# Mixture-of-experts forward pass: paired weight loads, and the head of x loaded ahead of the section

## The chip, the cores and the metric

The kernel runs on one core of a Trainium2 chip. Its time is device time in microseconds (us), taken as the median of several executions. A profile comes from one further execution; its span runs from the first to the last instruction and is a little shorter than the device time (179.5 against 181.1 us here).

The engines that matter are TensorE (matmuls, "PE" in the profile, with its weight loads as "PEld"), VectorE ("DVE"), ScalarE ("ACT"), GpSimd ("POOL") and SyncE ("SP"). GpSimd and SyncE issue the transfers between HBM (the chip's main memory) and SBUF (the on-chip memory of 128 partitions). Matmul results land in PSUM, from which VectorE and ScalarE copy them.

## The reference

Eight experts, each a two-layer network on its own 256 tokens:

```python
n_experts, capacity, hidden, expert_hidden = 8, 256, 512, 2048
# x [8, 256, 512], w1 [8, 512, 2048], w2 [8, 2048, 512], all float32
h = np.matmul(x, w1)
h = np.maximum(h, 0)
return np.matmul(h, w2).astype(np.float32)
```

The weights are 67.1 MB, x and the output 4.2 MB each.

## The kernel before

The tuned kernel keeps four slots for w1 and four for w2 in SBUF. GpSimd issues all weight loads and lets the transfer cast them from fp32 to bf16. One load is the w1 or the w2 of one expert (2 MB of bf16, 4.19 MB read from HBM); only the w2 of the last expert is cut in halves. The first half-stage is the transposition of x on TensorE: x lies for that time in the slot which w2 of expert 2 takes later. A quarter of x, its head, goes through SyncE as fp32 and is cast by VectorE; the rest is loaded and cast by GpSimd's transfer.

Everything stands in one critical section, in which the kernel places its own semaphores:

```python
E, C, H = x.shape; F = w1.shape[2]       # 8, 256, 512; 2048
MC = C // P; K1 = H // P; K2 = F // P    # 2, 4, 16
NS = 4                                   # slots of w1, and of w2
GJ, UG = 4, 2; NG = K2 // GJ             # hidden columns go in groups of 4 blocks, two PSUM buffers

loads = []
for e in range(E - 1):
    loads += [(1, e, 0, 2), (2, e, 0, 2)]
loads += [(1, E - 1, 0, 2), (2, E - 1, 0, 1), (2, E - 1, 1, 1)]
d_w = [sem(f"d_w{i}") for i in range(len(loads))]

with tc.tile_critical(no_gpsimd_drain=True):
    sp = nc.sync
    sp.dma_start(x_head[:], x_v[:, :HEAD * H]).then_inc(d_head, 16)
    for i, (w, e, h, n) in enumerate(loads):      # SyncE passes landings on as credits
        sp.wait_ge(d_w[i], 16)
        if w == 1: sp.sem_inc(c_w1, 1)
        else:      sp.sem_inc(c_w2, n)
    sp.wait_ge(v_last, MC)
    sp.dma_start(out_v[:, E - 1, :], ...).then_inc(d_last, 16)

    pool = nc.gpsimd
    pool.dma_start(x_sb[:, HEAD * H:], x_v[:, HEAD * H:]).then_inc(d_x, 16)
    # [cut: identity]
    for i, (w, e, h, n) in enumerate(loads):
        old = e - NS
        if (w, e) == (2, 2):
            pool.wait_ge(p_xt, K1 * MC)           # x has been transposed
        if old >= 0 and h == 0:                   # the slot's old expert is done
            if w == 1: pool.wait_ge(p_h, NG * (old + 1))
            else:      pool.wait_ge(p_o, MC * (old + 1))
        if i == len(loads) - 1:
            pool.wait_ge(v_out, 1)
            pool.dma_start(out_v[:16, 0:5:2, :16], ...).then_inc(d_first, 16)
        # [cut: src and dst of this load]
        pool.dma_start(dst, src).then_inc(d_w[i], 16)
    pool.wait_ge(v_out, 2)
    pool.wait_ge(d_first, 16)
    pool.dma_start(out_v[:, :E - 1, :], ...).then_inc(d_out, 16)   # experts 0 to 6

    dve = nc.vector
    dve.memset(identity[:], 0.0).then_inc(s_zero)
    dve.wait_ge(d_head, 16)
    dve.tensor_copy(x_sb[:, :HEAD * H], x_head[:]).then_inc(s_cast)
    # [cut: copies of the transposes, and of each expert's output from o_ps to out_sb]

    act = nc.scalar
    # [cut: copies of transposes; ReLU of each group, h_ps to hT; last output copy]
    act.wait_ge(d_out, 16)
    act.wait_ge(d_last, 16)
```

TensorE runs a loop over the experts. An expert has a first pass (w1, in two rounds of a loop of 32 matmuls) and a second pass (w2, 32 matmuls). It takes one credit of w1 before the first pass and one credit of w2 before each half of the second:

```python
def expert():
    take(c_w1, 1)
    loop("half", reg["half"], 2, half)      # h_ps <- xT, w1
    for k in range(K2):
        if k % JH == 0:
            take(c_w2, 1)
        # [cut: addresses]
        for m in range(MC):
            ...                             # o_ps[m] <- w2, hT; the last of each m increments p_o
```

The next expert's first pass follows the last matmul of this one directly if its credit is there.

Of the kernel before, what the change touches and what calls it, by code (L numbers as in the profile page):

```python
# [8 lines left out]
FP32 = mybir.dt.float32  # L9
BF16 = mybir.dt.bfloat16  # L10
PE = mybir.EngineType.PE

FIRST_FREE = 16512


@with_exitstack
def kernel(
# [7 lines left out]
    nc = tc.nc  # L25
    P = 128
    E, C, H = x.shape
    F = w1.shape[2]
    MC = C // P
    K1 = H // P  # L30
# [4 lines left out]
    HEAD = 4  # L35

    NS = 4
# [3 lines left out]
    UG = 2  # L41
    NG = K2 // GJ

    JH = K2 // 2
# [4 lines left out]
    x_v = x.rearrange("e (pp r) k -> (e pp) (r k)", r=R)  # L49
    w1_v = w1.rearrange("e (p ko) n -> p e (ko n)", ko=K1)  # L50
    w2_v = w2.rearrange("e (p h j) n -> p e h (j n)", h=2, j=JH)
    out_v = out.rearrange("e (p mo) k -> p e (mo k)", mo=MC)


    places, free = {}, FIRST_FREE

    def allot(name, shape, dtype):
        nonlocal free
        places[name] = free
        t = nc.alloc_sbuf_tensor_at(name, shape, dtype, offset=free)  # L60
        free += math.prod(shape[1:]) * mybir.dt.size(dtype)
        return t

    w1_sb = allot("w1_sb", [P, NS, K1 * F], BF16)
    w2_sb = allot("w2_sb", [P, NS, K2 * H], BF16)
    xT = allot("xT", [P, K1, MC, E * P], BF16)
    hT = allot("hT", [P, K2, C], BF16)
    out_sb = allot("out_sb", [P, E, MC, H], FP32)
    x_head = allot("x_head", [P, HEAD * H], FP32)
    identity = allot("identity", [P, P], BF16)  # L70
    W1_AT, W2_AT, XT_AT = places["w1_sb"], places["w2_sb"], places["xT"]

    x_sb = w2_sb[:, 2, :]
    X_AT = W2_AT + 2 * K2 * H * 2
# [5 lines left out]
    def sem(name):  # L80
        return tc.alloc_semaphore(name)


    d_head, d_x = sem("d_head"), sem("d_x")
    d_first, d_out, d_last = sem("d_first"), sem("d_out"), sem("d_last")

    s_zero, s_ident, s_cast = sem("s_zero"), sem("s_ident"), sem("s_cast")
    p_xt, p_h, p_o = sem("p_xt"), sem("p_h"), sem("p_o")
    v_out, v_last = sem("v_out"), sem("v_last")

# [1 line left out]
    c_h, c_o, c_w1, c_w2 = sem("c_h"), sem("c_o"), sem("c_w1"), sem("c_w2")  # L92


    loads = []
    for e in range(E - 1):
        loads += [(1, e, 0, 2), (2, e, 0, 2)]
    loads += [(1, E - 1, 0, 2), (2, E - 1, 0, 1), (2, E - 1, 1, 1)]
    d_w = [sem(f"d_w{i}") for i in range(len(loads))]

    with tc.tile_critical(no_gpsimd_drain=True):  # L101


        sp = nc.sync
        sp.dma_start(x_head[:], x_v[:, :HEAD * H]).then_inc(d_head, 16)
        for i, (w, e, h, n) in enumerate(loads):
            sp.wait_ge(d_w[i], 16)
            if w == 1:
                sp.sem_inc(c_w1, 1)
            else:  # L110
                sp.sem_inc(c_w2, n)
        sp.wait_ge(v_last, MC)
        sp.dma_start(
            out_v[:, E - 1, :], out_sb[:, E - 1].rearrange("p m h -> p (m h)")
# [1 line left out]


        pool = nc.gpsimd
        pool.dma_start(x_sb[:, HEAD * H:], x_v[:, HEAD * H:]).then_inc(d_x, 16)  # L119
        pool.wait_ge(s_zero, 1)  # L120

        pool.affine_select(  # L122
            out=identity[:],
# [4 lines left out]
            pattern=[[-1, P]],  # L128
            channel_multiplier=1,
        ).then_inc(s_ident)  # L130
        for i, (w, e, h, n) in enumerate(loads):


            old = e - NS
            if (w, e) == (2, 2):
                pool.wait_ge(p_xt, K1 * MC)
            if old >= 0 and h == 0:
                if w == 1:
                    pool.wait_ge(p_h, NG * (old + 1))
                else:  # L140
                    pool.wait_ge(p_o, MC * (old + 1))
            if i == len(loads) - 1:


                pool.wait_ge(v_out, 1)
                pool.dma_start(  # L146
                    out_v[:16, 0:5:2, :16], out_sb[:16, 0:5:2, 0, :16]
                ).then_inc(d_first, 16)
            if w == 2:
                src = w2_v[:, e, h:h + n, :].rearrange("p h n -> p (h n)")  # L150
                dst = w2_sb[:, e % NS, h * JH * H:(h + n) * JH * H]
            else:
                src, dst = w1_v[:, e, :], w1_sb[:, e % NS, :]
            pool.dma_start(dst, src).then_inc(d_w[i], 16)  # L154
        pool.wait_ge(v_out, 2)
        pool.wait_ge(d_first, 16)
        pool.dma_start(  # L157
            out_v[:, :E - 1, :], out_sb[:, :E - 1].rearrange("p e m h -> p e (m h)")
        ).then_inc(d_out, 16)
        pool.drain()  # L160

# [5 lines left out]


        dve = nc.vector
        dve.memset(identity[:], 0.0).then_inc(s_zero)  # L172
        dve.sem_inc(c_xt[0], 1)
        dve.sem_inc(c_o, MC)
        dve.wait_ge(d_head, 16)
        dve.tensor_copy(x_sb[:, :HEAD * H], x_head[:]).then_inc(s_cast)  # L176
        for ko in range(K1):
            dve.wait_ge(p_xt, ko * MC + 1)
            copy_xt(dve.tensor_copy, ko, 0).then_inc(c_xt[0])
# [10 lines left out]

        act = nc.scalar
        act.sem_inc(c_xt[1], 1)
        act.sem_inc(c_h, UG)
        for ko in range(K1):
            act.wait_ge(p_xt, ko * MC + 2)
            copy_xt(act.copy, ko, 1).then_inc(c_xt[1])
# [9 lines left out]
                ).then_inc(c_h)  # L206
        act.wait_ge(p_o, E * MC)
        act.copy(out_sb[:, E - 1, 1, :], o_ps[1][:]).then_inc(v_last)  # L208
        act.wait_ge(d_out, 16)
        act.wait_ge(d_last, 16)  # L210

# [1 line left out]
        pe = nc.tensor  # L215

        def take(s, n):
            pe.wait_ge(s, n).then_inc(s, -n)  # L218

        def at(t, reg, free):  # L220
            row = math.prod(t.shape[1:])
            return mybir.RegisterAccessPattern(
                ap=[[row, P], *free],
                dtype=BF16,
                memsetref=f"{t.name}_set",
                regref=reg.name,
                is_regloc_offset=False,
                reg_ap_offset=reg.name,
                const_ap_offset=0,
                const_sub_tensor_id=0,  # L230
            )

        def matmul(dst, weights, moving, **flags):
            inst = mybir.InstMatmult(
                name=nc.get_next_instruction_name(),
                engine=PE,
                ins=[moving, weights],
                outs=[pe.lower_ap(dst)],
                tile_size=(P, P),
                tile_position=(0, 0),  # L240
                **flags,
            )
            return pe.add_instruction(inst)  # L243

        def loop(name, counter, times, body):
            head, end = f"{name}_head", f"{name}_end"
            nc.br(head, engines=[PE])
            with nc.body(head, valid_engines=[PE]):
                body()
                pe.br_lt(counter, times, on_true=head, on_false=end)  # L250
            nc.switch_bb(end)

        reg = {
            n: pe.alloc_register(n)
            for n in ["count", "half", "slot", "x", "b1", "b2"]
            + [f"xt{ko}" for ko in range(K1)]
            + [f"a{i}" for i in range(12)]
        }
        bank = [[reg[f"a{b * 6 + i}"] for i in range(6)] for b in range(2)]

        def last_column(step):

            return (P - 1) * step * 2

        count = reg["count"]

        n = MC * (R // MC)

        def transposes():
            i = 0  # L270
            for m in range(MC):
                take(c_xt[m], 1)
                for r2 in range(R // MC):
                    if i % 6 == 0:
                        for k in range(i, min(i + 6, n)):
                            row = (k % (R // MC)) * MC + k // (R // MC)
                            pe.reg_add(bank[i // 6 % 2][k - i], reg["x"], row * H * 2)
                        if i + 6 > n:
                            pe.reg_add(reg["x"], reg["x"], 2)
                            pe.reg_add(count, count, 1)  # L280
                    t = matmul(
                        xt_ps[m][:, r2, :],
                        at(w2_sb, bank[i // 6 % 2][i % 6], [[K1, P]]),
                        pe.lower_ap(identity[:]),
                        start_tensor_calc=True,
                        stop_tensor_calc=True,
                        is_transpose=True,
                    )
                    i += 1
                t.then_inc(p_xt)  # L290

        pe.wait_ge(s_ident, 1)
        pe.wait_ge(s_cast, 1)
        pe.wait_ge(d_x, 16)
        pe.reg_mov(count, 0)
        pe.reg_mov(reg["x"], X_AT + last_column(K1))
        loop("transposes", count, K1, transposes)
        for m in range(MC):
            pe.wait_ge(c_xt[m], 1)

# [30 lines left out]
        def first_addresses():  # L331
            a, b, regs = CHUNKS1[0]
            compute(address1, range(a, b), regs)
# [76 lines left out]
        for ko in range(K1):  # L410
            pe.reg_add(reg[f"xt{ko}"], count, XT_AT + ko * MC * E * P * 2)
        first_addresses()
        take(c_h, 1)
        loop("expert", count, E, expert)


# [28 lines left out]
```

## Time and profile before

The time is 181.12 us, the median of 3 executions (181.11 to 181.21).

| From the page | Value |
|---|---|
| Span | 179.5 us, granted TensorE clock 0.961 |
| VectorE, ScalarE, GpSimd busy | 9%, 22%, 7% |
| Weight loads, issued by GpSimd | 15 of 2 MB and 2 of 1 MB |
| GpSimd's queue, share of the 16 transfer engines' time | 96.9% |
| SyncE's queue (head of x, store of expert 7) | 2.3% |
| Chain that ended last | 9% of the span, expert 7's matmuls, then one ScalarE copy |

How to read the lines in the next section. In a line of the page or of the groups, "x15" is a count. In the page's rows of 40 slices, each digit is the busy share of one slice (4.5 us here) in tenths. A timeline line gives the start in us, the duration in us, the engine, the line of the kernel, the operation and its tiles, the count of merged instructions, and in brackets the idle time before and what ended it. A line with "DMA to landing" gives the time from a transfer's issue to its last byte's arrival. A line of a table of stretches gives the stretch, its length, the busy time of PE, PEld, DVE, ACT and POOL, the granted clock (1.00 is full), the share of the transfer engines and GB/s. GB/s counts bytes as written, so a casting load shows half of what it reads.

### The profile page before, as it was taken

What the parts mean: (1) busy time and instruction counts of PE and PEld (TensorE: products, weight loads), DVE (VectorE), ACT (ScalarE), POOL (GpSimd) and SP (SyncE); (2) the same over time, 40 slices, a digit from 0 to 9 for tenths busy, and PEclk for the clock granted to TensorE, in tenths of its full rate; (3) what the DMA queues carried; (4) which work ended last, traced back from release to release, by engine and by line L of the source; (5) the groups of instructions that cost most, each with busy time, mean ns of one, the idle gap of its engine ahead of it and who ended that gap; (6) DMA issues with size and microseconds to landing.
All of it is one profiled execution on the core that took longest, in us unless ns stands there. A gap on an engine that the chain in (4) does not pass through costs nothing. (4 is left out here: it accounts for less than half of the span.)

```text
span 179.5 us, 2103 instructions
## 1 busy us (share of the span) xinstructions
PE 130.4 (73%) x824; PEld 90.9 (51%) x832; DVE 15.9 (9%) x21; ACT 38.7 (22%) x38; POOL 11.7 (7%) x25
## 2 busy tenths in 40 slices
PE   0007659997949794949778698949894968769980
PEld 0007548746924493418633495428741963359630
DVE  0203420002000200020002000020002000200010
ACT  2002423500520044003500044003600350004410
POOL 7100030101010101010101000020000000002000
PEclk9999999999987999999999699996999999969999
DMA  5999999999999999999999999999999999999995
GB/s 186 261 203 226 230 208 204 234 215 197 230 226 212 204 230 215 197 234 226 193 223 230 208 204 234 215 197 230 226 212 204 230 215 201 230 201 211 351 423 217
DMA packets 3824, 40.37 MB, mean 225 GB/s; under 512 B 368, under 2 KB 368, under 8 KB 1392
## 3 DMA queue, kind: packets, MB, share of 16 engines
q0 software_dynamic: 3536, 38.80, 96.9%
q1 hardware_dynamic: 288, 1.57, 2.3%
HBM read 71.30 MB, written 4.20 MB: 421 GB/s over the span
## 5 line engine op out<-in xcount | busy, mean ns | idle before, releaser
L243 PE MATMUL h_ps<-xT,w_sb 128*128 x512 | 65.2, 292 | 17.1 <-PEq L218 17.1
L243 PEld LDWEIGHTS h_ps<-xT,w_sb 128*128 x512 | 59.5, 147 | 24.7 <-issue 21.7
L243 PE MATMUL o_ps<-w_sb,hT 128*128 x248 | 57.8, 387 | 11.0 <-PEq L218 10.6
L202 ACT ACTIVATE hT<-h_ps 128x1024 bf16<-128x1024 f32 x32 | 32.8, 1024 | 111.3 <-PE h_ps L243 111.3
L243 PEld LDWEIGHTS o_ps<-w_sb,hT 128*128 128x128 bf16 x256 | 24.9, 99 | 41.6 <-issue 14.0
L185 DVE COPY out_sb<-o_ps 128x512 f32<-128x512 f32 x15 | 9.7, 686 | 141.4 <-PE o_ps L243 141.4
L243 PE MATMUL xt_ps<-identity,w_sb 128*128 128x128 bf16 x64 | 7.6, 310 | 16.0 <-PEq L218 16.0
L243 PEld LDWEIGHTS xt_ps<-identity,w_sb 128*128 x64 | 6.5, 145 | 16.8 <-issue 16.8
L154 POOL DMA_DIRECT2D w_sb<-in_w_dram x17 | 9.1, 542 | 87.7 <-PE o_ps L243 34.5
L165 ACT COPY xT<-xt_ps 128x1024 bf16<-128x1024 bf16 x4 | 4.0, 1012 | 18.2 <-PE xt_ps L243 18.2
L165 DVE COPY xT<-xt_ps 128x1024 bf16<-128x1024 bf16 x4 | 4.9, 1224 | 11.9 <-PE xt_ps L243 11.9
L157 POOL DMA_DIRECT2D out_dram<-out_sb x1 | 0.9, 950 | 44.3 <-DMA out_dram<-out_sb 44.3
L208 ACT COPY out_sb<-o_ps 128x512 f32<-128x512 f32 x1 | 0.6, 586 | 5.9 <-PE o_ps L243 5.9
L146 POOL DMA_DIRECT2D out_dram<-out_sb x1 | 0.6, 557 | 20.0 <-DVEq L188 20.0
L176 DVE CAST w_sb<-x_head 128x2048 bf16<-128x2048 f32 x1 | 1.2, 1227 | 4.8 <-DMA x_head<-in_x_dram 4.8
L165 ACT ACT_TABLE_LOAD x1 | 1.3, 1283 | 1.1 <-SPq L101 1.1
L119 POOL DMA_DIRECT2D w_sb<-in_x_dram x1 | 0.7, 682 | 1.0 <-DVE identity L172 1.0
L122 POOL TENSOR_SCALAR_AFFINE_SELECT identity<-identity 128x128 bf16<-128x128 bf16 x1 | 0.3, 305 | 0.1
L172 DVE MEMSET identity<- 128x64 uint32 x1 | 0.1, 112 | 1.0 <-SPq L101 1.0
L429 POOL MEMSET const-float32-0.0<- 128x1 f32 x1 | 0.1, 99 | 0.2 <-issue 0.2
L429 POOL MEMSET const-bfloat16-1.0<- 128x1 bf16 x1 | 0.1, 102 | 0.0
L429 POOL MEMSET const-uint8-127<- 128x1 uint8 x1 | 0.1, 102 | 0.0
(1 smaller groups left out, 0.1 us busy)
## 6 DMA issues: line engine op xcount, KB each, us to landing
w_sb<-in_w_dram POOLq DMA_DIRECT2D x15, 2048.0 KB, 65.7
out_dram<-out_sb POOLq DMA_DIRECT2D x1, 3584.0 KB, 12.9
w_sb<-in_w_dram POOLq DMA_DIRECT2D x2, 1024.0 KB, 57.1
w_sb<-in_x_dram POOLq DMA_DIRECT2D x1, 1536.0 KB, 11.7
x_head<-in_x_dram SPq DMA_DIRECT2D x1, 1024.0 KB, 5.0
out_dram<-out_sb SPq DMA_DIRECT2D x1, 512.0 KB, 3.0
out_dram<-out_sb POOLq DMA_DIRECT2D x1, 3.0 KB, 44.8
```

Source lines behind the costliest of these rows:

```text
L119: pool.dma_start(x_sb[:, HEAD * H:], x_v[:, HEAD * H:]).then_inc(d_x, 16)
L122: pool.affine_select(out=identity[:], in_=identity[:], compare_op=mybir.AluOpType.not_equal, fill=1.0, base=0, pattern=[[-1, P]], channel_ ...
L146: pool.dma_start(out_v[:16, 0:5:2, :16], out_sb[:16, 0:5:2, 0, :16]).then_inc(d_first, 16)
L154: pool.dma_start(dst, src).then_inc(d_w[i], 16)
L157: pool.dma_start(out_v[:, :E - 1, :], out_sb[:, :E - 1].rearrange("p e m h -> p e (m h)")).then_inc(d_out, 16)
L165: return copy(xT[:, ko, m].rearrange("k (ep r2) -> k ep r2", r2=R // MC), xt_ps[m][:].rearrange("k r2 ep -> k ep r2"),)
L176: dve.tensor_copy(x_sb[:, :HEAD * H], x_head[:]).then_inc(s_cast)
L185: cp = dve.tensor_copy(out_sb[:, e, m, :], o_ps[m][:])
L202: act.activation(hT[:, g * GJ:(g + 1) * GJ, :].rearrange("p a c -> p (a c)"), h_ps[g % UG][:], mybir.ActivationFunctionType.Relu,).then_in ...
L208: act.copy(out_sb[:, E - 1, 1, :], o_ps[1][:]).then_inc(v_last)
L243: return pe.add_instruction(inst)
L429: nc = _bacc.Bacc("TRN2", target_bir_lowering=False, num_devices=1)
```

## The change

The change has five parts.

- The head of x is loaded and cast ahead of the critical section, as an ordinary tile under the Tile framework, which places the waits itself. GpSimd's own wait for it stands at the load that overwrites x.
- The weights of experts 0 to 5 go partly two experts per transfer: w1 and w2 of 0 and 1, w1 and w2 of 2 and 3, w1 of 4 and 5. That makes 12 weight loads instead of 17. A pair waits for the slot of its second expert, and both experts' credits come when the whole pair has landed.
- Landings are counted on one semaphore for each slot, and GpSimd's other transfers share one semaphore.
- The identity matrix is zeroed by GpSimd instead of VectorE.
- ScalarE's waits for the final stores stand last in the section, and TensorE begins with one ScalarE credit less instead of taking it.

Its purpose is fewer transfers, semaphores and instructions, and an earlier start of the first load. The arithmetic is unchanged.

```diff
-    loads = []
-    for e in range(E - 1):
-        loads += [(1, e, 0, 2), (2, e, 0, 2)]
-    loads += [(1, E - 1, 0, 2), (2, E - 1, 0, 1), (2, E - 1, 1, 1)]
-    d_w = [sem(f"d_w{i}") for i in range(len(loads))]
+    loads = []
+    for es in [(0, 1), (2, 3)]:
+        loads += [(1, es, 0, 2), (2, es, 0, 2)]
+    loads += [(1, (4, 5), 0, 2), (2, (4,), 0, 2), (2, (5,), 0, 2)]
+    for e in range(6, E - 1):
+        loads += [(1, (e,), 0, 2), (2, (e,), 0, 2)]
+    loads += [(1, (E - 1,), 0, 2), (2, (E - 1,), 0, 1), (2, (E - 1,), 1, 1)]
+    # [cut: landed[i], the semaphore and count of load i]
+    x_head = x_pool.tile([P, HEAD * H], FP32, tag="x_head")
+    nc.sync.dma_start(x_head[:], x_v[:, :HEAD * H])
+    nc.vector.tensor_copy(x_sb[:, :HEAD * H], x_head[:])
     with tc.tile_critical(no_gpsimd_drain=True):
         sp = nc.sync
-        sp.dma_start(x_head[:], x_v[:, :HEAD * H]).then_inc(d_head, 16)
-        for i, (w, e, h, n) in enumerate(loads):
-            sp.wait_ge(d_w[i], 16)
-            if w == 1:
-                sp.sem_inc(c_w1, 1)
-            else:
-                sp.sem_inc(c_w2, n)
+        for i, (w, es, h, n) in enumerate(loads):
+            sp.wait_ge(*landed[i])
+            sp.sem_inc((c_w1, c_w2)[w - 1], n * len(es) if w == 2 else len(es))
 # [cut]
         pool = nc.gpsimd
-        pool.dma_start(x_sb[:, HEAD * H:], x_v[:, HEAD * H:]).then_inc(d_x, 16)
-        pool.wait_ge(s_zero, 1)
+        pool.dma_start(x_sb[:, HEAD * H:], x_v[:, HEAD * H:]).then_inc(d_pool, 16)
+        pool.memset(identity[:], 0.0).then_inc(s_ident)
+        pool.wait_ge(s_ident, 1)
 # [cut]
-            old = e - NS
-            if (w, e) == (2, 2):
+            old = es[-1] - NS
+            if w == 2 and 2 in es:
+                tc.wait_critical_data_deps()
                 pool.wait_ge(p_xt, K1 * MC)
 # [cut]
+            e, ne, at_slot = es[0], len(es), es[0] % NS
             if w == 2:
-                src = w2_v[:, e, h:h + n, :].rearrange("p h n -> p (h n)")
-                dst = w2_sb[:, e % NS, h * JH * H:(h + n) * JH * H]
+                src = w2_v[:, e:e + ne, h:h + n, :].rearrange("p e h n -> p e (h n)")
+                dst = w2_sb[:, at_slot:at_slot + ne, h * JH * H:(h + n) * JH * H]
             else:
-                src, dst = w1_v[:, e, :], w1_sb[:, e % NS, :]
-            pool.dma_start(dst, src).then_inc(d_w[i], 16)
+                src, dst = w1_v[:, e:e + ne, :], w1_sb[:, at_slot:at_slot + ne, :]
+            pool.dma_start(dst, src).then_inc(landed[i][0], 16)
 # [cut]
-        act.sem_inc(c_h, UG)
+        act.sem_inc(c_h, UG - 1)
-        act.wait_ge(d_out, 16)
-        act.wait_ge(d_last, 16)
 # [cut]
-        take(c_h, 1)
         loop("expert", count, E, expert)
+        pool.drain()
+        act.wait_ge(d_pool, 48)
+        act.wait_ge(d_last, 16).then_inc(s_ident)
```

More of the change, by code (lines that the diff above doesn't have):

```diff
@@ L11 @@
 PE = mybir.EngineType.PE
-FIRST_FREE = 16512
+FIRST_FREE = 16512 + 8192
 @with_exitstack
@@ L68 @@
     out_sb = allot("out_sb", [P, E, MC, H], FP32)
-    x_head = allot("x_head", [P, HEAD * H], FP32)
     identity = allot("identity", [P, P], BF16)
@@ L81, in sem @@
         return tc.alloc_semaphore(name)
-    d_head, d_x = sem("d_head"), sem("d_x")
-    d_first, d_out, d_last = sem("d_first"), sem("d_out"), sem("d_last")
-    s_zero, s_ident, s_cast = sem("s_zero"), sem("s_ident"), sem("s_cast")
+    d_w1 = [sem(f"d_w1{i}") for i in range(NS)]
+    d_w2 = [sem(f"d_w2{i}") for i in range(NS)]
+    d_half, d_pool, d_last = sem("d_half"), sem("d_pool"), sem("d_last")
+    s_ident = sem("s_ident")
     p_xt, p_h, p_o = sem("p_xt"), sem("p_h"), sem("p_o")
@@ L95 @@
     loads = []
-    for e in range(E - 1):
-        loads += [(1, e, 0, 2), (2, e, 0, 2)]
-    loads += [(1, E - 1, 0, 2), (2, E - 1, 0, 1), (2, E - 1, 1, 1)]
-    d_w = [sem(f"d_w{i}") for i in range(len(loads))]
+    for es in [(0, 1), (2, 3)]:
[4 more added lines that the diff above has]
+    loads += [(1, (E - 1,), 0, 2), (2, (E - 1,), 0, 1), (2, (E - 1,), 1, 1)]
+    landed, counts = [], {}
+    for w, es, h, _ in loads:
+        s = d_half if h else (d_w1, d_w2)[w - 1][es[0] % NS]
+        counts[id(s)] = counts.get(id(s), 0) + 16
+        landed.append((s, counts[id(s)]))
+    x_pool = ctx.enter_context(tc.tile_pool(name="x_pool", bufs=1))
+    x_head = x_pool.tile([P, HEAD * H], FP32, tag="x_head")
+    nc.sync.dma_start(x_head[:], x_v[:, :HEAD * H])
+    nc.vector.tensor_copy(x_sb[:, :HEAD * H], x_head[:])
     with tc.tile_critical(no_gpsimd_drain=True):
         sp = nc.sync
-        sp.dma_start(x_head[:], x_v[:, :HEAD * H]).then_inc(d_head, 16)
-        for i, (w, e, h, n) in enumerate(loads):
-            sp.wait_ge(d_w[i], 16)
-            if w == 1:
-                sp.sem_inc(c_w1, 1)
-            else:
-                sp.sem_inc(c_w2, n)
+        for i, (w, es, h, n) in enumerate(loads):
+            sp.wait_ge(*landed[i])
+            sp.sem_inc((c_w1, c_w2)[w - 1], n * len(es) if w == 2 else len(es))
         sp.wait_ge(v_last, MC)
@@ L130 @@
         ).then_inc(s_ident)
-        for i, (w, e, h, n) in enumerate(loads):
-            old = e - NS
-            if (w, e) == (2, 2):
+        for i, (w, es, h, n) in enumerate(loads):
+            old = es[-1] - NS
+            if w == 2 and 2 in es:
+                tc.wait_critical_data_deps()
                 pool.wait_ge(p_xt, K1 * MC)
@@ L147 @@
                     out_v[:16, 0:5:2, :16], out_sb[:16, 0:5:2, 0, :16]
-                ).then_inc(d_first, 16)
+                ).then_inc(d_pool, 16)
+            e, ne, at_slot = es[0], len(es), es[0] % NS
             if w == 2:
-                src = w2_v[:, e, h:h + n, :].rearrange("p h n -> p (h n)")
-                dst = w2_sb[:, e % NS, h * JH * H:(h + n) * JH * H]
-            else:
-                src, dst = w1_v[:, e, :], w1_sb[:, e % NS, :]
-            pool.dma_start(dst, src).then_inc(d_w[i], 16)
+                src = w2_v[:, e:e + ne, h:h + n, :].rearrange("p e h n -> p e (h n)")
+                dst = w2_sb[:, at_slot:at_slot + ne, h * JH * H:(h + n) * JH * H]
+            else:
+                src, dst = w1_v[:, e:e + ne, :], w1_sb[:, at_slot:at_slot + ne, :]
+            pool.dma_start(dst, src).then_inc(landed[i][0], 16)
         pool.wait_ge(v_out, 2)
-        pool.wait_ge(d_first, 16)
+        pool.wait_ge(d_pool, 32)
         pool.dma_start(
             out_v[:, :E - 1, :], out_sb[:, :E - 1].rearrange("p e m h -> p e (m h)")
-        ).then_inc(d_out, 16)
-        pool.drain()
+        ).then_inc(d_pool, 16)
         def copy_xt(copy, ko, m):
@@ L171 @@
         dve = nc.vector
-        dve.memset(identity[:], 0.0).then_inc(s_zero)
         dve.sem_inc(c_xt[0], 1)
         dve.sem_inc(c_o, MC)
-        dve.wait_ge(d_head, 16)
-        dve.tensor_copy(x_sb[:, :HEAD * H], x_head[:]).then_inc(s_cast)
         for ko in range(K1):
@@ L279, in transposes @@
                             pe.reg_add(reg["x"], reg["x"], 2)
-                            pe.reg_add(count, count, 1)
                     t = matmul(
@@ L290, in transposes @@
                 t.then_inc(p_xt)
[L292 to L297, printed above, removed]
+        pe.wait_ge(s_ident, 2)
+        pe.wait_ge(d_pool, 16)
+        x_first = X_AT + last_column(K1)
+        pe.reg_mov(reg["x"], x_first)
+        loop("transposes", reg["x"], x_first + K1 * 2, transposes)
         for m in range(MC):
```

## The prediction

> **What bounds the kernel now.** I read the page first (shares of busy time, the 40 slices, the HBM line), then the TensorE timeline, then single weight loads with their time to landing, then a table of stretches for the tail.
>
> From the page:
>
> ```profile
> PE 130.4 (73%) x824; PEld 90.9 (51%) x832; DVE 15.9 (9%) x21; ACT 38.7 (22%) x38; POOL 11.7 (7%) x25
> DMA  5999999999999999999999999999999999999995
> HBM read 71.30 MB, written 4.20 MB: 421 GB/s over the span
> w_sb<-in_w_dram POOLq DMA_DIRECT2D x15, 2048.0 KB, 65.7
> ```
>
> No compute engine is full, but the DMA row is at 9 in every slice except the first and the last. The last line says how: a 2 MB weight load (4.19 MB of fp32 in HBM, cast on the way) lands a median 65.7 us after it was issued, so it waits in the queue behind six or so others. The queue never runs dry.
>
> From two single loads (the w1 loads of experts 5 and 7) and the TensorE timeline:
>
> ```profile
> L154 POOL DMA_DIRECT2D w_sb<-in_w_dram x1: 531/531/531, 50.1 to 50.1; - x1
> DMA to landing us min/median/max: 69.6/69.6/69.6
> ...
> L154 POOL DMA_DIRECT2D w_sb<-in_w_dram x1: 531/531/531, 88.8 to 88.8; - x1
> DMA to landing us min/median/max: 69.6/69.6/69.6
> ```
>
> ```profile
> 119.89 8.85 PE L243 MATMUL h_ps<-xT,w_sb 128*128 x64 [2.67 <-PEq L218]
> 129.53 7.07 PE L243 MATMUL o_ps<-w_sb,hT 128*128 x31 [0.79 <-PEq L218]
> 139.23 7.38 PE L243 MATMUL h_ps<-xT,w_sb 128*128 x64 [2.63 <-PEq L218]
> 148.91 7.07 PE L243 MATMUL o_ps<-w_sb,hT 128*128 x31 [2.31 <-PEq L218]
> 158.64 8.94 PE L243 MATMUL h_ps<-xT,w_sb 128*128 x64 [2.66 <-PEq L218]
> 167.47 7.07 PE L243 MATMUL o_ps<-w_sb,hT 128*128 x31
> ```
>
> Issue plus time to landing gives 50.1 + 69.6 = 119.7 us and 88.8 + 69.6 = 158.4 us. TensorE starts those experts 0.2 us later, at 119.89 and 158.64. Four loads lie between, so one takes 38.7 / 4 = 9.69 us (433 GB/s of reads). An expert costs 19.4 us of transfer but only about 14.5 us of TensorE (7.38 + 7.07), so TensorE starts each half the moment its weights land.
>
> The tail, by stretches (the two last columns are the DMA share and GB/s):
>
> ```profile
> 168.00:176.00 8.00, 6.54 (x30) 2.74 (x28) 0.69 (x1) 1.23 (x2) 0.00 (x0) 1.00 1.02 419
> 176.00:178.00 2.00, 0.00 (x0) 0.00 (x0) 0.00 (x0) 0.00 (x0) 0.00 (x0) 1.00 0.71 289
> ```
>
> The last half of w2 lands at 119.2 + 49.0 = 168.2 us. From there the transfers stay full to 176 us with the stores of experts 0 to 6, and the store of expert 7 follows at once: issued at 175.18, landed 3.0 us later at 178.2. So the chain of waits, which ends in TensorE and a ScalarE copy, misleads: behind expert 7's matmuls the transfers are still busy with 3.67 MB of other stores. The kernel is one unbroken stream of transfers from about 2 to 178 us, plus about 1.3 us of closing barrier.
>
> **What the Trainium skill says.** "DMA: Bandwidth & Descriptors", section "Where 436 GB/s comes from", puts the ceiling of the 16 ports at 435 GB/s; the 433 GB/s above agrees, so the stream has no room. Its section "Issuing engines are not separate DMA queues" says that SyncE's and GpSimd's transfers share the same 16 engines; the tail agrees, as expert 7's store runs when the others end. Its section "Latency and other measured facts" reports half the rate for copies between HBM tensors when neighbouring rows lie 4 MiB apart. The paired loads alternate between two experts 4 MiB apart; no run here shows whether that counts. "TensorE: Matmul & The Clock Gate", Part 1, says that an idle window of about 3.4 us halves the clock until about 3.4 us of work have passed. The trace agrees in size: a slow first pass takes 8.9 us instead of 7.38, but it also occurs after idle times of only 2.7 us, and not after all of them.
>
> **The change, part by part.**
>
> (1) Head of x by Tile, ahead of the section. SyncE now issues this load before the section's opening handshake. In the trace it left at 0.95 us, after a no-op and a branch which released the other engines at about 0.8 us. I take 0.2 us off. Everything in the stream stands behind this load, so all landings move 0.2 us earlier. The price is that TensorE, ScalarE, VectorE and SyncE now enter the section when the head has landed and VectorE has cast it (5.9 + 1.2 = 7.1 us). TensorE has nothing to do before the rest of x has landed (1.4 + 11.7 = 13.1 us), so this costs nothing. GpSimd does not wait at entry, only before the w2 load that overwrites x, where it waits for the transposes anyway. The identity's zeroing moves to GpSimd (0.1 us on VectorE), behind its first DMA issue; the weights it delays need not start before about 12.5 us. Value: -0.2 us.
>
> (2) Pairs. Seventeen weight issues become twelve, at about 0.54 us each on an engine busy 7%: nothing. Bytes and order are the same apart from the swap inside a pair. Counting 9.69 us a load from x at 13.1, and without the shift: w1 of 0 and 1 lands at 32.5 (expert 0 had it at 22.9), w2 of 0 and 1 at 51.9, w1 of 2 and 3 at 71.3, their w2 at 90.6, w1 of 4 and 5 at 110.0, w2 of 4 at 119.7, of 5 at 129.4, then as before: 139.1, 148.7, 158.4, 163.3, 168.2.
>
> TensorE then: expert 0 first pass 32.7 to 41.6 (slow clock), second pass 52.1 to 60.8; expert 1 has all its weights, 61.0 to 75.5; expert 2 first pass 75.6 to 83.0, wait, second pass 90.8 to 99.5 (slow clock, 8.75 as at 52 us in the kernel before). From there it has a backlog and works at 14.6 us an expert (7.38 + 7.07 and an estimated 0.15 for the turn): expert 3 ends at 114.1, 4 at 128.7, 5 at 143.3, 6 at 157.9. Expert 7 can't start before its w1 at 158.4 + 0.2. So the backlog of about 10 us is worked off with some 0.7 us to spare. If TensorE is late by one or two us there, its clock stays up and expert 7 takes 7.38 instead of 8.94 us, which pays 1.6 us back.
>
> Buffers: the pair of w1 4 and 5 waits for expert 1's first pass, about 68.3 us, while the queue has work to 90.6: 22 us in hand, the tightest case. w2 of 6 waits for expert 2's end, 99.5 against 139.1; w2 of 7 for expert 3's, 114.1 against 158.4. The stream doesn't break. Value: 0.
>
> (3) Credits per expert, one starting credit less, and a shared semaphore for GpSimd's transfers: the same waits in other bookkeeping. Value: 0.
>
> (4) ScalarE waits last. Its two waits end at the same landing at 178.2; one branch after them goes away. Value: -0.1 us.
>
> Sum: 181.12 - 0.2 - 0.1 = 180.8 us.
>
> **The rivals.**
>
> (A) The late start of TensorE costs. For it: the first matmul of an expert moves from 25.4 to 32.7 us, the second pass from 34.3 to 52.1. Were TensorE the bound, that would add 7 to 10 us. Against it: 19.4 against 14.6 us an expert, four experts to catch up in, and 1.6 us from the clock. Moreover the stream ends at 178 whatever TensorE does, as long as expert 7's store has been issued by about 175.2. If my turn is too short (say 16 us an expert), expert 7 starts near 164 and ends near 178.6: about 185 us.
>
> (B) The paired loads run slower, because a partition's two rows lie 4 MiB apart. For it: the skill's page. Against it: that figure is for every partition's row 4 MiB away from its neighbour's; here partitions stay 32 KB apart and only the two blocks of 32 KB in one partition are far apart. And the store of seven experts is such a form itself (7 pieces for each partition) and ran at 419 GB/s. Ten loads of 9.69 us are in pairs; 3% on those is 2.9 us, 184 us.
>
> (C) TensorE finishes earlier, since its clock stays up before expert 7, and the time falls by 1.6 us. Against it: the stores of the tail are in the same stream; an earlier store of expert 7 only shares the engines with the others. The tail stretch leaves 0.29 x 2.0 = 0.6 us of idle DMA at most: 180.3 us.
>
> (D) Larger transfers run closer to the peak. Against it: landings are already evenly spaced at 433 GB/s, with the next load always queued. Nothing to gain.
>
> **Range and chances.** The stream leaves little room down: 0.3 us for the start and end, up to 0.5 from the tail. Upwards, A and B in small form give up to 1 us. So 80% between 180.2 and 181.9 us. Faster by over 2% would need 177.5 us, below what the bytes allow: 2%. Slower by over 2% needs 184.7 us, so A or B in full: 5%. Within 2%: 93%.
>
> **What would show it.** Head of x issued at about 0.75 us; w1 of 7 landing near 158.2 us; the DMA row at 9 throughout; TensorE waiting long (about 10 and 8 us) before the second passes of experts 0 and 2, then hardly at all from 91 to 157 us, and shortly before expert 7; seven-expert store issued near 164 us. I am wrong if the w1 of 7 lands later than in the kernel before (B), if expert 7 starts well after its weights (A), or if the stream has a hole.

## The result, and the profile after

| | Time, us (median, range) | Ratio to before, 95% interval |
|---|---|---|
| Before | 181.12 (181.04 to 181.81) | |
| Changed | 180.61 (180.51 to 180.84) | 0.9967 (0.9952 to 0.9983) |

The changed kernel is 0.5 us, 0.3%, faster. Predicted were 180.8 us.

From the page of the changed kernel:

```profile
PE 129.4 (72%) x832; PEld 90.5 (51%) x832; DVE 15.8 (9%) x20; ACT 38.7 (22%) x38; POOL 10.3 (6%) x21
DMA  6999998999999999899899999999989999999995
HBM read 71.30 MB, written 4.20 MB: 422 GB/s over the span
w_sb<-in_w_dram POOLq DMA_DIRECT2D x5, 4096.0 KB, 48.0
w_sb<-in_w_dram POOLq DMA_DIRECT2D x5, 2048.0 KB, 51.0
```

The DMA row still has no hole. Some digits are 8, but the rate (422 against 421 GB/s) is what counts: the transfers are as full as before.

The start, from the timelines of the kernel before (two lines) and of the changed kernel (two lines), and the changed kernel's w1 load of expert 7 (its issue, and its time to landing):

```profile
0.95 0.38 SPq L105 DMA_DIRECT2D x_head<-in_x_dram  x1
1.44 0.68 POOL L119 DMA_DIRECT2D w_sb<-in_x_dram  x1 [1.00 <-DVE identity L172]
0.74 0.38 SPq L116 DMA_DIRECT2D x_head<-in_x_dram  x1
1.24 0.68 POOL L131 DMA_DIRECT2D w_sb<-in_x_dram  x1 [0.79 <-POOLq L440]
```

```profile
L169 POOL DMA_DIRECT2D w_sb<-in_w_dram x1: 528/528/528, 107.1 to 107.1; - x1
DMA to landing us min/median/max: 51.0/51.0/51.0
```

The head of x leaves at 0.74 instead of 0.95 us. The w1 of expert 7 lands at 107.1 + 51.0 = 158.1 instead of 158.4 us.

TensorE's timeline:

```profile
32.39 9.24 PE L252 MATMUL h_ps<-xT,w_sb 128*128 x64 [9.20 <-PEq L227]
51.74 9.73 PE L252 MATMUL o_ps<-w_sb,hT 128*128 x32 [10.11 <-PEq L227]
61.30 7.35 PE L252 MATMUL h_ps<-xT,w_sb 128*128 x64
68.54 7.07 PE L252 MATMUL o_ps<-w_sb,hT 128*128 x32
75.44 7.34 PE L252 MATMUL h_ps<-xT,w_sb 128*128 x64
90.44 9.15 PE L252 MATMUL o_ps<-w_sb,hT 128*128 x32 [7.66 <-PEq L227]
99.43 7.34 PE L252 MATMUL h_ps<-xT,w_sb 128*128 x64
...
113.57 7.35 PE L252 MATMUL h_ps<-xT,w_sb 128*128 x64
120.80 7.07 PE L252 MATMUL o_ps<-w_sb,hT 128*128 x32
127.70 7.35 PE L252 MATMUL h_ps<-xT,w_sb 128*128 x64
...
149.07 7.07 PE L252 MATMUL o_ps<-w_sb,hT 128*128 x32
158.22 8.85 PE L252 MATMUL h_ps<-xT,w_sb 128*128 x64 [2.08 <-PEq L227]
166.96 7.07 PE L252 MATMUL o_ps<-w_sb,hT 128*128 x32
```

It shows a wait of 9.2 us for the first pair, the two long waits before second passes (10.1 and 7.7 us, in the brackets), then lines without brackets, which are back-to-back work on the backlog, and a wait of 2.1 us before expert 7. With its weights there, an expert takes 127.70 - 113.57 = 14.13 us.

The tail, in the stretches of the prediction:

```profile
168.00:176.00 8.00, 6.03 (x28) 2.53 (x26) 0.69 (x1) 0.72 (x2) 0.00 (x0) 1.00 1.03 422
176.00:178.00 2.00, 0.00 (x0) 0.00 (x0) 0.00 (x0) 0.00 (x0) 0.00 (x0) 0.65 0.53 215
```

In 168 to 176 us the stores run at much the same rate as before (422 against 419 GB/s), and they finish a little sooner: 215 instead of 289 GB/s are left in the last stretch.

### The profile page after: what moved, and what is told of

It is laid out like the page before. It is cut to its first block, busy times and chain, and to the rows that moved or that the text cites. A ratio compares the mean times of both kernels' runs of the same rounds, so it can differ in the third digit from the quotient of the medians.

```text
span 178.9 us, 2103 instructions
## 1 busy us (share of the span) xinstructions
PE 129.4 (72%) x832; PEld 90.5 (51%) x832; DVE 15.8 (9%) x20; ACT 38.7 (22%) x38; POOL 10.3 (6%) x21
## 5 line engine op out<-in xcount | busy, mean ns | idle before, releaser
L252 PE MATMUL o_ps<-w_sb,hT 128*128 x256 | 61.3, 401 | 17.8 <-PEq L227 17.8
L252 PE MATMUL h_ps<-xT,w_sb 128*128 x512 | 62.2, 284 | 11.3 <-PEq L227 11.3
L252 PEld LDWEIGHTS h_ps<-xT,w_sb 128*128 x512 | 58.4, 146 | 15.9 <-issue 13.1
L252 PEld LDWEIGHTS o_ps<-w_sb,hT 128*128 128x128 bf16 x256 | 25.6, 102 | 50.7 <-issue 24.5
L169 POOL DMA_DIRECT2D w_sb<-in_w_dram x12 | 7.4, 619 | 105.1 <-PE h_ps L252 58.0
```

Of the source, the lines that this page charges most:

```text
L169: pool.dma_start(dst, src).then_inc(landed[i][0], 16)
```

## The experiments

Each run was compared with the kernel before on the same chip. My theory was the stream of transfers: what doesn't move its start, its length or the closing doesn't move the time. The rivals were TensorE, and the pairs themselves. One result, that of the first experiment, needed a further theory.

| Run | Time, us | Before, us | Ratio, 95% interval |
|---|---|---|---|
| Head of x alone | 181.96 | 181.12 | 1.0039 (1.0025 to 1.0053) |
| Pairs alone | 181.03 | 181.12 | 0.9996 (0.9990 to 1.0003) |
| Waits at the end alone | 181.17 | 181.12 | 1.0001 (0.9993 to 1.0009) |
| Changed, less TensorE work | 180.68 | 181.12 | 0.9977 (0.9970 to 0.9984) |
| Changed, two more pairs | 186.23 | 181.07 | 1.0281 (1.0261 to 1.0302) |
| Before, head issued late | 182.41 | 181.07 | 1.0070 (1.0053 to 1.0087) |
| Head and credit | 181.01 | 181.13 | 0.9994 (0.9988 to 1.0001) |
| Before, one TensorE wait more | 182.22 | 181.13 | 1.0054 (1.0038 to 1.0069) |
| Changed, bf16 store | 180.61 | 181.13 | 0.9970 (0.9963 to 0.9977) |
| Changed, pairs undone | 180.76 | 181.08 | 0.9981 (0.9974 to 0.9988) |
| Changed, waits put back | 180.88 | 181.08 | 0.9990 (0.9981 to 0.9998) |
| Changed, 22 semaphores more | 180.81 | 181.08 | 0.9986 (0.9978 to 0.9995) |

### Is the end set by TensorE or by the transfers?

Less TensorE work, in the changed kernel. Seven of 16 blocks of every second pass are left out, so this is not the full computation:

```diff
                 for m in range(MC):
+                    if k % 2 and k != K2 - 1:
+                        continue
                     mm = matmul(o_ps[m][:], ...)
```

> The changed kernel, leaving out the matmuls of 7 of the 16 blocks in every second pass (14 of 32 matmuls, 3.0 us of TensorE for each expert); its output is therefore not the reference's. TensorE ends near 171 instead of 174 us and the store of expert 7 is issued near 171.7 us. My theory (the transfers set the end): time 180.3 to 180.6 us. Rival (the chain of waits is right and TensorE's last expert sets the end): 177.6 us.

Measured: 180.68 us. The last two TensorE lines and the last store of its timeline, then its store line from the page (the last column is us to landing), and below them the same store in the changed kernel:

```profile
158.02 8.65 PE L252 MATMUL h_ps<-xT,w_sb 128*128 x64 [5.64 <-PEq L227]
166.56 4.05 PE L252 MATMUL o_ps<-w_sb,hT 128*128 x17
...
171.26 0.35 SPq L125 DMA_DIRECT2D out_dram<-out_sb  x1
```

```profile
out_dram<-out_sb SPq DMA_DIRECT2D x1, 512.0 KB, 6.4
```

```profile
174.67 0.35 SPq L125 DMA_DIRECT2D out_dram<-out_sb  x1
...
out_dram<-out_sb SPq DMA_DIRECT2D x1, 512.0 KB, 3.1
```

Expert 7's store leaves at 171.26 instead of 174.67 us, 3.4 us sooner, and then takes 6.4 instead of 3.1 us to land, beside the other stores (which land 0.5 us later than in the changed kernel, at 177.0 us). It lands at 177.6 us, much as in the changed kernel (177.8). The chain of waits of the page named the last matmuls and was wrong: they are not what the end hangs on.

Two more pairs, in the changed kernel:

```diff
-    loads += [(1, (4, 5), 0, 2), (2, (4,), 0, 2), (2, (5,), 0, 2)]
-    # [cut: w1 and w2 of expert 6, w1 of expert 7]
+    loads += [(1, (4, 5), 0, 2), (2, (4, 5), 0, 2)]
+    loads += [(1, (6, 7), 0, 2), (2, (6,), 0, 2)]
```

> The changed kernel with two more pairs: w2 of experts 4 and 5, and w1 of experts 6 and 7. The bytes and the stream's length stay. By the model with which I predicted: w2 of 4 and 5 lands near 129.0 us, so expert 4's second pass starts there (slow clock, to 138.4); experts 5 and 6 follow without a pause to 152.6 and 166.8, expert 7 to 181.0 us; its store is issued at 181.6 and lands at 184.7, time 187.4 us. Rival (only the stream sets the end, whatever TensorE does): 180.6 us.

Measured: 186.23 us. Its timeline:

```profile
129.03 0.58 PE L251 MATMUL o_ps<-w_sb,hT 128*128 x1 [8.39 <-PEq L226]
129.83 7.62 PE L251 MATMUL o_ps<-w_sb,hT 128*128 x30 [0.22 <-issue]
137.29 7.35 PE L251 MATMUL h_ps<-xT,w_sb 128*128 x64
...
172.80 7.07 PE L251 MATMUL o_ps<-w_sb,hT 128*128 x31
...
180.51 0.35 SPq L124 DMA_DIRECT2D out_dram<-out_sb  x1
```

So TensorE does set the end once a pair comes too late to work off its delay. The whole delay comes from the first of the two pairs, w2 of 4 and 5: after the wait of 8.4 us for it there is no further wait. Expert 4's second pass starts at 129.03 us as computed. The model was 1.1 us too slow in that pass alone: I had it end at 138.4 us by the slow clock, and the next pass began at 137.29. The three experts behind it took 14.2 us each (137.29 to 179.87 us), as expected here.

### What sets the start of the stream?

The kernel before, with the head issued late:

```diff
         dve.memset(identity[:], 0.0).then_inc(s_zero)
+        dve.memset(out_sb[:, 0:6]..., 0.0).then_inc(s_late)
# ...
+        sp.wait_ge(s_late, 1)
         sp.dma_start(x_head[:], x_v[:, :HEAD * H]).then_inc(d_head, 16)
```

> The kernel before, with the head's load made to wait for a zeroing of the output buffer on VectorE, which delays its issue by some 3 to 6 us. The zeroing is overwritten later. If the head alone sets the start of the stream and GpSimd's first transfer follows it, the hole is filled as soon as GpSimd's data can flow: the end moves by the time from 1.9 us to GpSimd's first packet. If GpSimd's queue is ready about 1 us after its issue ended (near 3 us), the time is about 182.2 us; if it isn't ready before 4.85 us, where its packets began in the kernel before, about 184 us. Rival (the start doesn't matter): 181.1 us.

Measured: 182.41 us. Two lines of its timeline, SyncE's and TensorE's first pass of expert 0:

```profile
7.58 0.38 SPq L107 DMA_DIRECT2D x_head<-in_x_dram  x1
...
37.55 9.99 PE L246 MATMUL h_ps<-xT,w_sb 128*128 x64 [1.88 <-PEq L221]
```

The head left 6.6 us late, and expert 0 started 12 us later than in the kernel before, but the time rose by only 1.3 us. In the trace, GpSimd's first packet moved at 2.83 us, where the head's had moved at 1.95: 0.9 us. The rows of the first 5 us, in slices of 0.125 us, first of the kernel before and then of this run:

```profile
DMA  0000000000000009993083959769699796969999
DMA  0000000000000000000000999967000000509999
```

The last landing came 1.1 us later. So 0.9 of the 1.3 us are the later first packet of the stream, whoever sends it. What the remaining 0.4 us are stays open (the second row also has a hole from about 3.5 to 4.3 us). TensorE's start, 12 us later, can have cost no more than these.

### The parts alone

The head of x alone, with the identity zeroed by GpSimd:

```diff
-        sp.dma_start(x_head[:], x_v[:, :HEAD * H]).then_inc(d_head, 16)
+    x_head = x_pool.tile([P, HEAD * H], FP32, tag="x_head")
+    nc.sync.dma_start(x_head[:], x_v[:, :HEAD * H])
+    nc.vector.tensor_copy(x_sb[:, :HEAD * H], x_head[:])
```

> The kernel before with one part of the change: the head of x loaded by Tile ahead of the section (and the identity zeroed by GpSimd, which goes with it); weights stay one expert per transfer. My theory (one unbroken stream of transfers, whose start this load sets): head issued near 0.74 us instead of 0.95, w1 of expert 7 landing near 158.1 instead of 158.4 us, time 180.8 to 180.9 us, 0.2 to 0.3 below before. Rival (the gain comes from the pairs): 181.1 us.

Measured: 181.96 us, 0.8 above before, which neither theory had. Yet the head left at 0.74 us, w1 of expert 7 landed at 158.1 us, and the span was shorter: a median of 179.1 against 179.3 us. The loss lies behind the span. Time less span is 2.86 us, against 1.78 in the kernel before. The list of transfers after the span's end shows two that carry instructions, of 16 and 8 KB; the kernel before has none there.

The pairs alone, the same lines of the diff as in the change:

> The kernel before with the pairs alone; the head of x, the identity and the waits at the end stay as before. My theory: TensorE starts expert 0 near 32.7 us instead of 25.4 and catches up before expert 7; w1 of 7 lands within 0.15 us of before; time 181.0 to 181.1 us. Rival (fewer, larger transfers shorten the stream): 180.8 us or less. Rival (two experts 4 MiB apart slow the loads): above 181.5 us.

Measured: 181.03 us, not told apart from before by this run. TensorE started expert 0 at 32.46 us and was waiting again for expert 7, which it began at 158.30 us. No sign of slower pairs.

The waits at the end alone:

```diff
         loop("expert", count, E, expert)
+        pool.drain()
+        act.wait_ge(d_out, 16)
+        act.wait_ge(d_last, 16).then_inc(s_ident)
```

> The kernel before with only GpSimd's drain and ScalarE's two waits moved to the end of the section. My theory: everything up to the last landing is unchanged, one branch less after it: time 181.0 us, 0.1 below before. Rival (the whole gain of the end comes from there): 180.8 us.

Measured: 181.17 us. The span is 0.1 us shorter (median 179.2), but the time behind it is 0.15 us longer (1.93), so nothing is left.

### The microsecond behind the span

The head alone adds one instruction each to the programs of TensorE, SyncE and ScalarE, and three to GpSimd's: 129 in the listing of TensorE's program instead of 128. The changed kernel has 127. The credit that TensorE no longer takes saves one. A second one goes by a part of the change that its list doesn't name: the loop over the transposes counts with its address register, so that no separate counter is set. I added the credit to the head alone:

```diff
-        act.sem_inc(c_h, UG)
+        act.sem_inc(c_h, UG - 1)
# ...
-        take(c_h, 1)
         loop("expert", count, E, expert)
```

> The run with the head of x alone, plus the credit of the change (ScalarE gives one credit less at the start and TensorE doesn't take it): one TensorE instruction less, as many as in the kernel before; SyncE and GpSimd keep their one and three instructions more than before. The head alone gave a span 0.2 us shorter but a time 0.8 us longer, and its trace has an instruction transfer of 16 KB after the span that the kernel before hasn't. Theory (TensorE's program grew by one instruction over a boundary of its instruction memory, and the end of the program pays for it): the extra microsecond goes, time 180.7 to 180.9 us. Rival (SyncE's or GpSimd's program, or Tile's tile itself, costs it): 181.9 to 182.0 us.

And, in the kernel before, one TensorE wait that has nothing to wait for:

```diff
         pe.wait_ge(s_cast, 1)
+        pe.wait_ge(s_zero, 1)
         pe.wait_ge(d_x, 16)
```

> The kernel before with one redundant TensorE wait, on a semaphore that has long been reached; nothing else changes, and it stands before the transposes where TensorE waits for x anyway. Theory (instruction memory of TensorE): span as before, 179.3 to 179.5 us, time 182.0 to 182.2 us, 0.9 to 1.1 more. Rival: 181.1 us, as before.

Measured: 181.01 us with the credit, 182.22 us with the needless wait. The span of the latter is 179.3 us as a median, as before; time less span is 2.87 us. The list of transfers of this kernel from 179.6 to 183 us, behind its span (queue, kind, count, MB, share):

```profile
DMA packets 2, 0.02 MB, mean 7 GB/s; under 512 B 0, under 2 KB 0, under 8 KB 0
q8 instruction: 1, 0.02, 2.4%
q14 instruction: 1, 0.01, 0.9%
```

The same stretch of the kernel before, from 179 us on:

```profile
DMA packets 0, 0.00 MB, mean 0 GB/s; under 512 B 0, under 2 KB 0, under 8 KB 0
```

The 129th TensorE instruction costs 1.09 us, and it comes with a fetch of 16 KB of instructions behind the span, which takes 1.33 us in this trace (1.43 us in that of the head alone). The twelve other kernels have no transfer there, and 1.7 to 1.9 us behind their spans. That the time waits for this fetch is the reading that fits; no run separates the two. The Trainium skill, "Runtime: NRT & Kernel Launch", section "Instruction fetch mechanics", has blocks of 16 KiB (256 instructions) and says that crossing a boundary is mostly hidden. The size agrees with the trace; by this reading it is not hidden in these two kernels, where it falls at the end. That it is TensorE's program is shown, as nothing else was changed. How the listing's 128 instructions, of which 80 are matmuls that run as a weight load and a matmul, come to a full block is not; what is added when the program is loaded isn't in the listing.

### Taking parts away from the changed kernel

The parts alone gave -0.12 (head and credit), -0.09 (pairs) and +0.05 us (waits), less than the 0.5 us together. So I took parts away one at a time (no run takes away the head, the credit or the transposes' counter).

The pairs undone:

```diff
-    for es in [(0, 1), (2, 3)]:
-        loads += [(1, es, 0, 2), (2, es, 0, 2)]
-    # [cut: the pair of w1 of 4 and 5]
+    for e in range(E - 1):
+        loads += [(1, (e,), 0, 2), (2, (e,), 0, 2)]
```

> The changed kernel with the pairs undone: every weight load is of one expert, all else as changed. The traces so far have 145.20 us from x's landing to that of the 15th expert's load in kernels with pairs against 145.35 without, so pairs would shorten the stream by 0.15 us. Theory (each part gives its small share and they add): 180.7 to 180.8 us. Rival (the pairs carry the gain that the parts run alone did not show): 181.0 us. Rival (pairs are worth nothing): 180.6 us.

The old place of the waits:

```diff
         act.copy(out_sb[:, E - 1, 1, :], o_ps[1][:]).then_inc(v_last)
+        act.wait_ge(d_pool, 48)
+        act.wait_ge(d_last, 16)
# [cut: the drain likewise; both leave the section's end]
```

> The changed kernel with ScalarE's waits and GpSimd's drain put back where they stood. Theory (moving them saves 0.1 us within the span): span 178.95, time 180.7 us. Rival (it is worth nothing or less, as in the run that moved them alone, where the time after the span grew by 0.15 us): 180.6 us or less.

Semaphores added:

```diff
+    spare = [sem(f"spare{i}") for i in range(22)]
     d_half, d_pool, d_last = sem("d_half"), sem("d_pool"), sem("d_last")
```

> The changed kernel with 22 semaphores more, unused; GpSimd's clearing of the semaphores at the end took 266 ns for 42 of them in the kernel before and 203 ns for 31 in the changed one, 5.7 ns each. Theory: the clearing takes about 330 ns, time 180.73 us, 0.13 more than the changed kernel. Rival (it is hidden): 180.6 us.

Measured: 180.76, 180.88 and 180.81 us; below the kernel before on that chip by 0.32, 0.20 and 0.27 us, where the whole change had 0.51. By the medians the pairs, the place of the waits and 22 semaphores are each worth 0.2 to 0.3 us here. But the changed kernel's own interval (0.9952 to 0.9983, which is +-0.28 us) overlaps those of all three, so these times are indications. I rely on what the traces of all the runs show of each part, which is finer:

- Pairs: from the landing of x to the landing of the w1 load of expert 7, six kernels with these pairs take 145.19 to 145.29 us, and six without 145.33 to 145.66 us (145.33 in the kernel before). The medians are 0.18 us apart. In GpSimd's queue the kernel before moves 320 packets of 4 bytes and the changed one 240, 16 fewer for each of the five joined transfers; the 80 took 0.11 us of each transfer engine's time. What the rest is, no run shows.
- Waits last: from the last landing to the start of GpSimd's clearing of semaphores, the seven kernels that have it take 0.66 to 0.68 us, the seven others 0.76 to 0.78 us: 0.10 us.
- Semaphores: the clearing took 266 ns for 42 of them in the kernel before, 203 for 31 in the changed one and 330 for 53 with the 22 added:

```profile
L440 POOLq EVENT_SEMAPHORE_RANGE_CLEAR  x1: 266/266/266, 178.9 to 178.9; - x1
L451 POOLq EVENT_SEMAPHORE_RANGE_CLEAR  x1: 203/203/203, 178.4 to 178.4; - x1
L452 POOLq EVENT_SEMAPHORE_RANGE_CLEAR  x1: 330/330/330, 178.4 to 178.4; - x1
```

- Head: the first packet moved at 1.74 instead of 1.95 us, 0.21 us sooner.

Added up, 0.21 + 0.18 + 0.10 + 0.06 = 0.55 us, against 0.51 measured. Single executions of one form differ by 0.1 to 0.3 us over the stretch of the first item, so the sum accounts for the size of the gain and doesn't prove each term in the time. Putting the waits back added 0.1 us behind the span (1.86 against 1.77 us), and moving them in the kernel before added 0.15 there, which I can't explain.

### An attempt at a faster version

Outputs of experts 0 to 6 kept as bf16 and cast by the store, which rounds them once more:

```diff
+    out_bf = allot("out_bf", [P, E - 1, MC, H], BF16)
# ...
-                cp = dve.tensor_copy(out_sb[:, e, m, :], o_ps[m][:])
+                cp = dve.tensor_copy((out_bf if e < E - 1 else out_sb)[:, e, m, :], o_ps[m][:])
```

> The changed kernel with the outputs of experts 0 to 6 kept as bf16 and cast to fp32 by the store, an attempt at a faster version that rounds the output once more. If a transfer engine's time goes by the bytes read (as with the casting loads, which read 4 and write 2 bytes at 433 GB/s of reads), the stores of 0 to 6 end near 172.3 us, and the store of expert 7 alone sets the end: issued at 173.2 to 174.7, landing 2.6 us later: time 178.7 to 180.2 us. If it goes by the larger of the two sides: 180.6 us, as the changed kernel.

Measured: 180.61 us, as the changed kernel. Half the bytes to read bring nothing: the store of experts 0 to 6 took 12.85 us to land, against 12.80 in the changed kernel, so here its time went by the 4 bytes written and not by those read. The timeline and the page also show the other point again:

```profile
158.22 7.38 PE L253 MATMUL h_ps<-xT,w_sb 128*128 x64 [1.44 <-PEq L228]
...
173.20 0.35 SPq L126 DMA_DIRECT2D out_dram<-out_sb  x1
```

```profile
out_dram<-out_sb SPq DMA_DIRECT2D x1, 512.0 KB, 4.6
```

Here expert 7 ran at the full clock and its store left 1.5 us sooner than in the changed kernel. It landed at 177.8 us all the same. No run beat the changed kernel.

## Why the prediction was right, and where it wasn't

**What bounds the kernel: right.** A stream from 1.7 us to 177.8 us; a last store issued 3.4 us sooner brings nothing, and the late head moves the end by 1.1 us, 0.9 of them the delay of the first packet.

**(1) The head of x: right in sign, and smaller by itself.** The issue moved by 0.21 us as predicted. The head with the credit gave 0.12 us in the time (interval from 0.02 us slower to 0.2 faster). That entering the section late costs nothing is confirmed: TensorE began the transposes at 13.37 us, earlier than the 13.74 before.

**(2) The pairs: the schedule right, its value off.** The landings came within 0.5 us of the list; the waits of about 10 and 8 us came as 10.1 and 7.7. "Value: 0" was wrong by a little: five transfers fewer shorten the stream by about 0.2 us, by the landings in the traces, of which packets of 4 bytes that go away can be 0.11 us. The step that failed was rival (D)'s dismissal, that evenly spaced landings leave nothing to gain: even spacing doesn't show what each boundary costs. Rival (B) is refuted: pairs of experts 4 MiB apart are not slower (one takes 19.35 us in the changed kernel, from 32.22 to 51.57 us, which is 433 GB/s of reads as before).

**TensorE's turn: mis-sized.** I took 14.6 us an expert, 7.38 + 7.07 + 0.15. It is 14.13: in the timeline each pass starts 0.1 to 0.2 us before the end of the one ahead of it; the spare time before expert 7 was 2.1 instead of 0.7 us. The hoped-for full clock in expert 7 came in the bf16 run, after 1.44 us of idling, and not in the profile of the changed kernel, after 2.08 us (8.85 us for the pass). It doesn't matter to the time either way, as rival (C)'s rebuttal said.

**(3) The credits: the waits are the same, but "Value: 0" left out two terms.** One is the number of TensorE instructions: the head of x alone brings it to 129 and costs 0.8 us net, and with the credit it doesn't. Nothing in the prediction counts instructions, so that the changed kernel stays under this step is luck. By the listing it would stay there, at 128, with the credit taken as before; no run has that. The other is the semaphores: 11 fewer to clear save 63 ns in the trace.

**(4) The waits at the end: -0.1 predicted.** Right within the span: from the last landing to ScalarE's last signal the trace shows 0.12 instead of 0.23 us, and the 0.10 us stand in all traces, as said above. In the time it was worth nothing alone and about 0.3 us in the changed kernel by the medians, with overlap as said above; the part behind the span stays open.

The sum of -0.3 us against -0.5 thus left out two small terms, pairs (0.2 us) and semaphores (0.06 us). It holds because the bound was read rightly, and because the one large term, the step of 1.09 us for a TensorE instruction, happened to stay out of the changed kernel.

## What to carry to other kernels

When transfers are full from end to end, ask of every part only whether it moves the first packet, the number of transfers or the closing. Here TensorE could start 7 us later for free, as its backlog was worked off before the last weights landed; with two more pairs it wasn't, and the kernel took 5.2 us longer than before. Compare the time with the span: what one instruction too many costs can lie behind the span, where no line of the page shows it. Test a part alone and also take it away from the whole, since a part that seems idle can be what makes another one affordable, as the credit did for the head of x alone.

## What the runs showed of the hardware that was not expected

- One redundant TensorE wait, the 129th instruction of the listing, cost 1.09 us, with a 16 KB instruction transfer after the span.
- The length of a pause alone doesn't tell whether the pass behind it is slow. In the kernel before, a pause of 2.66 us stands before a first pass of 7.38 us (at 81.15 us) and before one of 8.94 us (at 158.64). After 1.44 us the pass was fast in both cases (7.38 us, in the bf16 run and in the one with less TensorE work), after 2.08 us it took 8.85 us in the changed kernel.
- The head's load issued at 7.58 us beside a full GpSimd queue took 16.5 us to land, against 5.0 at the start.
- GpSimd's first packets moved at 2.83 us when no other transfer was in flight, and at 4.85 us behind the head's, though they were issued at the same 1.44 us.
- Clearing a semaphore at the end costs about 5.8 ns, (330 - 203) / 22.
